# Half of the condition's broadcast row, a fifth raw tile, and gate sums by halves

## The chip, the cores and the metric

The kernel runs on one core of a Trainium2 chip. Its time is the device time of one execution in microseconds (us); with more than one run, the median counts. A core has a matrix engine (PE in the profile), a vector engine (DVE), a scalar engine (ACT), a fourth engine (POOL) and an engine that here only issues transfers (SP). Each takes its instructions in the order of the program; they wait for one another through semaphores. Transfers that SP and POOL issue run on DMA engines beside them.

## The reference

One layer of an encoder: 512 positions, 2048 channels, float32. The condition `c` gives three rows of 2048 numbers (shift, scale, gate); the normalised input, scaled and shifted, goes through one large projection whose columns feed a windowed attention with 16 heads (`aq` to `ag`) and a gated linear attention (GLA) with 4 heads (`gq` to `gg`). Both are gated by a SiLU, joined, projected, multiplied by the gate row, added to the input and normalised. Cut to what matters here:

```python
mod = jax.nn.silu(c) @ w_cond[layer] + b_cond[layer]
shift, scale, gate = jnp.split(mod, 3, axis=-1)
h = rms_norm(x) * (1.0 + scale[:, None]) + shift[:, None]
proj = h @ w_in[layer]
aq, ak, av, ag, gq, gk, gv, gg, lr_f, lr_b = jnp.split(proj, PROJ_SPLITS, axis=-1)
...
a_out = att.reshape(B, S, ATT_WIDTH) * jax.nn.silu(ag)
...
g_out = g_o * jax.nn.silu(gg)
y = jnp.concatenate([a_out, g_out], axis=-1) @ w_out[layer]
x = x + gate[:, None] * y
return rms_norm(x) * final_gain
```

Two kinds of sums over 2048 channels matter for this case. The gate row is `silu(c) @ w_cond` for its 2048 columns. And where the shift goes through the projection of `ag`, it gives a row of its own, `shift @ W_ag`, a bias of 1024 numbers. Both are matrix times vector, and the kernel computes them on the vector engine, not on PE.

## The kernel before

The order of PE's instructions is written out by hand; a scheduler orders those of the other four engines. Every product in float32 is made of three matmuls of a high and a low part (L215 to L217: high by high, low by high, high by low), so each block of weights is loaded as raw float32, its high part is taken on ACT (`split_hi`, L442) and its low part on DVE (`split_lo`, L428).

**Stages.** A first stage reads the condition's weights and the first columns of the projection, and makes shift and scale on DVE with sums against `sb`, a tile of 128 partitions by 2048 that holds silu(c) in every partition. `sb` then stays for the gate sums, and near the end the finished gate row is loaded into the same tile. After the first stage the projection runs in units: qk2, qk4, qk6, gk, gv0, gv1, ag0, ag1, gg0, gg1. Each unit has eight blocks of weights (`qk65` is block 5 of unit qk6, `ag11` block 1 of ag1) and 64 ticks of six matmuls, and carries side work on the way: attention heads in the qk units and gk, GLA heads in gv1, ag0, ag1 and gg0 (heads 0 to 3). The out projection follows, from about 783 us on, in products of halves (`O` blocks).

**Side work of an attention head** (h, i: head and quarter, so s91 is quarter 1 of head 9): score on PE into a PSUM tile (L730, L731); on DVE the bias is added and the row's smallest value found (L734); exp on ACT (L737); reciprocal on DVE (L738); normalisation on POOL (L742); four transposes on PE (L754) into a PSUM tile; their high and low part on ACT (L758) and DVE (L759); values on PE (L768), added up by ACT (L771) and DVE (L775, `cat`). Scores, transposes, values and all GLA products draw PSUM tiles in turn from one ring of three (`PA`), so that each PE product waits until the reader of the tile three products back is done. t90 takes the tile of s91.

**Side work of a GLA head** (h, d: head and direction): z on PE (L869), gates on DVE and ACT (L875 to L899, ending in `ki` L898 and `qi` L899), transposes `kt` (L908), products `kv` (L920), states (L927, L932), attention (L947), mask (L952, L954), outputs `go` (L969), squares `gsq` (L974), their high part `gsh` on ACT (L981) and low part `gsl` on DVE (L982), the norm `gn` on PE (L983, L984), and the result `cat` on DVE (L992). At the end of a unit of ag or gg its four PSUM tiles are gated on DVE (L1052, L1050).

**The sums.** 16 of them give the bias (`rawv{m}{z}`, m 0 to 7) and 32 the gate (`rawg{m}{z}`, m 0 to 15), with z the half of the 2048 channels: each loads 512 KB from SP (L838, L804) and is one instruction on DVE (L843 for the bias' first half, L314 for the rest) that multiplies the raw tile by a broadcast row (`shb` for the bias, `sb` for the gate) and adds up. The sum of z = 1 goes on from the result of z = 0. `SUMS_IN` says how many run in which unit; `some_sums` puts the load of each a little ahead of its place. `masked` makes a gate sum wait, in the order, for the last mask (L954).

**Raw tiles.** The weight blocks (L359), the bias sums and the gate sums all take their raw tile from one ring of four (`RAW`, 128 x 1024). A load can start when the sum, or both splits, of the block four places back are done.

**Transfers of POOL.** Sums of blocks of the output weights are made in DRAM: `T<-in_w_o` and `T<-T` (L391), 512 KB each, of which some copy and some add. They are paced along the units.

Of the kernel before, what the change touches and what calls it, by code (L numbers as in the profile page):

```python
# [10 lines left out]
F32 = mybir.dt.float32  # L11
# [3 lines left out]
ALU = mybir.AluOpType  # L15
# [3 lines left out]
P = 128  # L19
S = 512  # L20
D = 2048
KT = D // P
# [89 lines left out]
GLA_AT = (0.01, 0.02, 0.33, 0.46, 0.46, 0.56, 0.64, 0.76, 0.76, 0.88)  # L112
GLA_FIRST = 0.2

SUMS_IN = {"qk6": 4, "gk": 4, "gv0": 9, "gv1": 2, "ag0": 7, "ag1": 9, "gg0": 9}


OUT_ORDER = ("P1", "P7", "P6", "P4", "P5", "P3", "P2")
# [60 lines left out]
def block_kernel(ctx: ExitStack, tc: tile.TileContext, a: dict):  # L179
    nc = tc.nc  # L180
    cst = ctx.enter_context(tc.tile_pool(name="cst", bufs=1))
# [3 lines left out]
    mid = ctx.enter_context(ExitStack())  # L185
    t2 = mid.enter_context(tc.tile_pool(name="t2", bufs=16))
    gp = mid.enter_context(tc.tile_pool(name="gp", bufs=2))
    sm = mid.enter_context(tc.tile_pool(name="sm", bufs=4))
    pp = ctx.enter_context(tc.tile_pool(name="pp", bufs=4, space=PSUM))
    dp = ctx.enter_context(tc.tile_pool(name="dp", bufs=1, space=DRAM))  # L190
    ctx.enter_context(tc.manual_schedule(engines={E.PE}))

    def T2(name, dt=F32, parts=P):
        return t2.tile([parts, 512], dt, tag="t2", name=name)
# [4 lines left out]
    def PJ(name):  # L199
        return pp.tile([P, 512], F32, tag="pj", bufs=5, name=name)  # L200
# [5 lines left out]
    tt = nc.vector.tensor_tensor  # L206
# [20 lines left out]
    bcond = cst.tile([P, 48], F32, tag="bcond", name="c_bcond")  # L227
# [17 lines left out]
    def RAW(name, shape):  # L245
        return wp.tile([P] + shape, F32, tag="raw", bufs=4, name=name)
# [18 lines left out]
        c = slice(512 * z, 512 * z + 512)  # L265
        nc.sync.dma_start(start_w["a", 0][:, c], a["w_sa"][0, :, 0, c])

    sb = cst.tile([P, 2048], F32, tag="sb", name="sb")
    hot = T2("hot", F32R)
    onesr = cst.tile([P, P], F32R, tag="ones", name="ones")  # L270
    ones = onesr.bitcast(F32)
# [40 lines left out]
    def cond_sum(dst, w, with_, init):  # L312

        nc.vector.tensor_tensor_reduce(out=w, in0=w, in1=with_, op0=ALU.mult, op1=ALU.add,  # L314
                                       scale=1.0, scalar=init, accum_out=dst)
# [98 lines left out]
    def block_sums(name):  # L414
        n = SUM_OPS_IN[name]
        r = [sum_ops.pop(0) for _ in range(n)]
        return [((q + 0.5) / n, x) for q, x in enumerate(r)]
# [13 lines left out]
    def split_hi(i):  # L431
        if i < len(groups) and i not in wts:
            fetch(i)
            u, g = groups[i]
            raw = raws[i].rearrange("p k c -> p (k c)")
            dst = None
            if (u, g) == ("O", len(groups) - gi["O", 0] - 4):
                t = b8.tile([P, 2, 1024], F32R, tag="b8", name="wlast")
                dst = t[:, 0, :], t[:, 1, :]
            wts[i] = dst or (wp.tile([P, 1024], F32R, tag="whi", name=f"{u}{g}h"),  # L440
                             wp.tile([P, 1024], F32R, tag="wlo", name=f"{u}{g}l"))
            last["hi"] = act(wts[i][0], raw, AF.Copy).ins  # L442
# [182 lines left out]
    for z in range(2):  # L625
        for e in range(3):
            name = ("mm", "a", 0, 7) if (z, e) == (1, 2) else ("m0", z, e)
# [3 lines left out]
    for i in range(n):  # L631
        if i > 7:
            mm_task(i)
        st, k, j = chain[i]
# [15 lines left out]
    for i in range(n, 2 * n):  # L650
        mm_task(i)
        st, k, j = chain[i]
# [3 lines left out]
    for w in range(4):  # L656
        for kt in range(4):
            j, g = w // 2 * 4 + kt, w % 2
# [20 lines left out]
    gate = cst.tile([P, KT], F32, tag="gate", name="gate")  # L679
    gate0 = cst.tile([P, KT], F32, tag="gate0", name="gate0")  # L680
# [117 lines left out]
    def gate_half(m, z):  # L798

        t = []  # L800

        def load():
            t.append(RAW(f"rawg{m}{z}", [1024]))
            nc.sync.dma_start(t[0], a["wg"][m, z])  # L804

        def go():
            raw = t[0]

            with tc.issue_after(masked[-1]) if masked else nullcontext():
                if z == 0:  # L810
                    cond_sum(gate0[:, m:m + 1], raw, sb[:, :1024], bcond[:, 32 + m:33 + m])
                else:
                    cond_sum(gate[:, m:m + 1], raw, sb[:, 1024:], gate0[:, m:m + 1])
        return load, go

    masked = []
# [15 lines left out]
    def bias_half(m, z):  # L832

        t = []

        def load():
            t.append(RAW(f"rawv{m}{z}", [1024]))
            nc.sync.dma_start(t[0], a["wv"][m, z])  # L838

        def go():  # L840
            raw = t[0]
            if z == 0:
                nc.vector.tensor_tensor_reduce(out=raw, in0=raw, in1=shb[0][:, :1024], op0=ALU.mult, op1=ALU.add,  # L843
                                               scale=1.0, scalar=0.0, accum_out=vbias0[:, m:m + 1])
            else:
                cond_sum(vbias[:, m:m + 1], raw, shb[0][:, 1024:], vbias0[:, m:m + 1])
        return load, go

    sum_work = [bias_half(m, z) for m in range(8) for z in range(2)]
    sum_work += [gate_half(m, z) for m in range(KT) for z in range(2)]  # L850

    def some_sums(name):
        r = [sum_work.pop(0) for _ in range(SUMS_IN.get(name, len(sum_work)))]
        n = len(r)
        loads = [(max(q - 0.3, 0.1) / n, x[0]) for q, x in enumerate(r)]
        return sorted(loads + [((q + 0.7) / n, x[1]) for q, x in enumerate(r)], key=lambda x: x[0])
# [144 lines left out]
    def urgent(go):  # L1001
        with tc.high_priority(offset=20):
            go()
# [3 lines left out]
    def unit(name, natural, side=(), lr=None):  # L1007
        side = sorted(spill + list(side) + block_sums(name), key=lambda x: x[0])
        spill[:] = [(at - 1, go) for at, go in side if at >= 1]
        side = [x for x in side if x[0] < 1]  # L1010
        ps = [PJ(f"ps_{name}_{i}") for i in range(4)]
        pos, tick, ticks = 0, 0, 64
        for g in range(KT // 2):
            i0 = gi[name, g]
            split_hi(i0)
            split_hi(i0 + 1)
            for ahead in (2, 3):
                fetch(i0 + ahead)
            split_lo(i0)
            hi, lo = wts[i0]  # L1020
            for i in range(4):
                for kk in range(2):
                    k = 2 * g + kk
                    rh, rl = h_hi[:, k, :], h_lo[:, k, :]
                    if natural:
                        t = slice(i * P, i * P + P)
                        cw = slice(kk * 512, kk * 512 + 512)
                        three(ps[i], rh[:, t], rl[:, t], hi[:, cw], lo[:, cw], k == 0, k == KT - 1)
                    else:
                        c = slice(kk * 512 + i * P, kk * 512 + i * P + P)  # L1030
                        three(ps[i], hi[:, c], lo[:, c], rh, rl, k == 0, k == KT - 1)
                    tick += 1
                    if tick % 8 == 2:
                        split_lo(i0 + 1)
                    while pos < len(side) and side[pos][0] * ticks <= tick:
                        urgent(side[pos][1])
                        pos += 1
                if lr is not None:
                    lr(4 * g + i)
        while pos < len(side):  # L1040
            urgent(side[pos][1])
            pos += 1
        return ps
# [9 lines left out]
        lnexp()  # L1053


    for p in range(2):
        qk_evict(p, psb["b", 4 + 2 * p], psb["b", 5 + 2 * p])
    for n, p in (("qk2", 0), ("qk4", 2), ("qk6", 4)):
        ps = unit(n, False, attention((p, p + 1)) + ([(0.05, shift_row)] + some_sums(n) if p == 4 else []))
        for q in range(2):  # L1060
            qk_evict(p + 2 + q, ps[2 * q], ps[2 * q + 1])

    ps = unit("gk", False, attention((6, 7)) + some_sums("gk"))
    gla["k"] = B8("gkt", [4, 512])
    for i in range(4):
        act(gla["k"][:, i, :], ps[i], AF.Copy)
# [18 lines left out]
    ps = unit("gv0", True, some_sums("gv0"), lr=lr_tick)  # L1085
# [20 lines left out]
    ps = unit("gv1", True, gla_head(0) + some_sums("gv1"))  # L1106
# [3 lines left out]
    for j in range(2):  # L1110
        ps = unit(f"ag{j}", False, gla_head(1 + j) + some_sums(f"ag{j}"))
        gate_evict(ps, cat[j], f"a{j}", vbias[:, 4 * j:4 * j + 4])
    ps = unit("gg0", False, gla_head(3) + some_sums("gg0"))
# [43 lines left out]
    ps = unit("gg1", False, side + some_sums("gg1"))  # L1157
# [4 lines left out]
    op = ctx.enter_context(tc.tile_pool(name="op", bufs=1, reuse_waits="tile"))  # L1162
    for e in "hl":
        t = hp.tile([P, KT, 512], F32R, tag="h", name="c_" + e)
        for z, n in enumerate(("S2", "A22", "S1", "S4")):
            ops.setdefault(n, []).append(
                t[:, 4 * z:4 * z + 4, :].rearrange("p k (two c) -> p (k two) c", two=2))

    def gate_row():

        pg = PA("pgate")
        nc.tensor.transpose(pg[:KT, :P], gate, ident)
        gt_ = E_("gatet")
        act(gt_[:KT, :P], pg[:KT, :P], AF.Copy)
        garow = dp.tile([KT, P], F32, tag="garow", name="garow")
        nc.sync.dma_start(garow, gt_[:KT, :P])
        nc.sync.dma_start(sb, bass.AP(garow.tensor, garow.offset, [[0, P], [1, D]]))

    def E_(name):
        return op.tile([P, 512], F32, tag="e", bufs=3, name=name)  # L1180
# [33 lines left out]
    def add_up(i, j, merge, gain):  # L1214

        x_ = xo[i, j]
        t = E_(f"y{i}{j}")
        merge(t)
        tt(t, t, sb[:, 512 * j:512 * j + 512], op=ALU.mult)
        tt(x_, t, x_, op=ALU.add)  # L1220
        act(t, x_, AF.Square, accum_out=ssq[:, i, j:j + 1])
        if gain:
            tt(x_, x_, fgain[j], op=ALU.mult)
# [204 lines left out]
```

## Time and profile before

| | us |
|---|---|
| median of 3 runs | 942.63 (942.31 to 943.21) |
| the profiled execution | 940.34 |
| its span in the profile | 938.6 |
| granted PE clock, mean | 0.994 |
| DVE, gate sums with `sb`, 16 + 16 | 20.5 + 20.5 busy, 1283 ns each |
| idle on DVE ahead of them | 31.1 + 19.1, nearly all for DMA |
| DVE, bias sums, 8 + 8 | 9.8 + 10.3 busy |
| idle on DVE ahead of them | 16.0 + 15.0, all for DMA |
| HBM read and written | 200.53 MB and 37.83 MB |

The profile is one execution. In its views a row has a start in us from the span's start, a duration, the engine, the line, the operation, and tiles written and read with buffer numbers left out; in square brackets stands the idle time ahead of it and what ended it. In the view of waits a row gives who waited for whom, the total, how often, and the longest. The chain of waits follows the execution back from its end, at each step to what released it. In the DMA views the last number is the time from issue to landing. A row of a stretch gives the stretch, its length, busy time and count of PE, PEld (weight loads), DVE, ACT and POOL, then the granted PE clock, the DMA share and GB/s.

### The profile page before, as it was taken

Reading aid. Unit: us, or ns where it says so; the run is one execution under the profiler, and the core shown is the slowest. Engines: PE = TensorE matmul, PEld = TensorE weight load, DVE = VectorE, ACT = ScalarE, POOL = GpSimd, SP = SyncE. Lnnn points to the kernel's source line nnn. Section 1 sums busy time; section 2 is a strip of 40 time slices with the busy share of each in tenths; the row PEclk is TensorE's granted clock in tenths of the full one; section 3 lists DMA queues with packets and bytes.
Section 4 is the critical chain, followed back from the end, with each engine's and each line's share of the span. In section 5 each row is a group of like instructions: output and inputs, shape, how many; then the busy total and the mean of one; then the engine's idle time right before and its main releaser. Section 6 shows DMA issues by size and latency. Waiting matters only on the chain.

```text
span 938.6 us, 12129 instructions
## 1 busy us (share of the span) xinstructions
PE 917.5 (98%) x4375; PEld 760.8 (81%) x4375; DVE 654.6 (70%) x960; ACT 472.2 (50%) x770; POOL 98.3 (10%) x152
## 2 busy tenths in 40 slices
PE   7999999999999999999999999989989999999996
PEld 6888888888888888888877888878878888888884
DVE  7988899766755676766444657476686639697496
ACT  5553533565655645655413545363643428555464
POOL 0000000012222122122000100111002000000001
PEclk9999999999999999999999999999999999999998
DMA  9999497465765775755656546666766567856743
GB/s 352 404 412 383 166 372 269 158 199 148 188 198 153 217 234 166 239 167 147 209 200 197 162 151 221 202 199 199 247 209 200 187 195 267 315 203 217 276 179 135
DMA packets 54339, 209.79 MB, mean 224 GB/s; under 512 B 7204, under 2 KB 7492, under 8 KB 45960
## 3 DMA queue, kind: packets, MB, share of 16 engines
q1 hardware_dynamic: 48656, 174.83, 51.1%
q0 software_dynamic: 5184, 33.62, 15.1%
q8 instruction: 34, 0.56, 0.2%
q10 hardware_dynamic: 440, 0.57, 0.2%
q14 instruction: 25, 0.20, 0.1%
HBM read 200.53 MB, written 37.83 MB: 254 GB/s over the span
## 4 chain that ended last, share of the span: by engine, by line
PE 81%; DMA 8%; DVE 7%; issue 3%; ACT 1%; POOL 0%; SPq 0%; DVEq 0%; POOLq 0%; ACTq 0%
DMA rawg<-in_wg 5%; PE ps_qk L215 4%; PE ps_qk L217 4%; PE ps_qk L216 4%; PE g L217 4%; PE g L215 4%; PE g L216 4%; PE stb L217 3%; PE stb L216 3%; PE stb L215 3%; PE o L768 3%; PE ps_gv L217 3%; PE ps_gv L216 3%; PE ps_gv L215 3%; PE t L754 3%
## 5 line engine op out<-in xcount | busy, mean ns | idle before, releaser
L737 ACT ACTIVATE p<-p,st 128x512 f32<-128x512 f32 x64 | 46.1, 720 | 56.3 <-DVE st L734 55.9
L314 DVE CUSTOM_DVE_ANT_0 cb<-cb,sb,c_bcond 128x2048 f32<-128x2048 f32 (+1 forms) x32 | 73.4, 2295 | 1.3 <-DMA cb<-in_wm 1.0
L391 POOL DMA_DIRECT2D T<-in_w_o x48 | 33.5, 704 | 311.3 <-ACT qk21h L442 119.8
L742 POOL TENSOR_SCALAR p<-p,st 128x512 f32<-128x512 f32 x62 | 43.2, 697 | 196.1 <-DVE st L738 152.9
L759 DVE TENSOR_TENSOR pt<-t,pt 128x512 fp32r<-128x512 f32 x64 | 43.7, 688 | 15.6 <-ACT pt L758 15.4
L734 DVE CUSTOM_DVE_ANT_0 p<-s,g 128x512 f32<-128x512 f32 x64 | 43.6, 686 | 13.7 <-PE s L731 13.4
L758 ACT ACTIVATE pt<-t 128x512 fp32r<-128x512 f32 x64 | 37.8, 591 | 9.9 <-PE t L754 8.9
L314 DVE CUSTOM_DVE_ANT_0 rawg<-rawg,sb,gate 128x1024 f32<-128x1024 f32 x16 | 20.5, 1283 | 31.1 <-DMA rawg<-in_wg 30.9
L754 PEld LDWEIGHTS t<-c_ident,p 128*128 128x128 f32 x256 | 31.5, 140 | 9.7 <-POOL p L742 1.4
L754 PE MATMUL t<-c_ident,p 128*128 128x128 f32 x256 | 38.5, 273 | 0.1
L768 PEld LDWEIGHTS o<-pt,vv 128*128 128x128 f32 x256 | 34.8, 188 | 2.8
L768 PE MATMUL o<-pt,vv 128*128 128x256 f32 x256 | 35.5, 281 | 0.0
L314 DVE CUSTOM_DVE_ANT_0 rawg<-rawg,sb,c_bcond 128x1024 f32<-128x1024 f32 x16 | 20.5, 1282 | 19.1 <-DMA rawg<-in_wg 19.0
L738 DVE RECIPROCAL st<-st 128x1 f32<-128x1 f32 x64 | 10.3, 161 | 24.9 <-ACT p L737 24.9
L730 PE MATMUL s<-ks,qs 128*128 128x512 f32 x64 | 25.1, 392 | 0.2 <-DVE cat L775 0.2
L731 PE MATMUL s<-kl,qs 128*128 128x512 f32 x64 | 25.0, 391 | 0.0
L937 ACT ACTIVATE sq<-st,sc 128x256 f32<-128x256 f32 x24 | 12.2, 508 | 22.1 <-DVE st L927 13.0
L843 DVE CUSTOM_DVE_ANT_0 rawv<-rawv,shb 128x1024 f32<-128x1024 f32 x8 | 9.8, 1225 | 16.0 <-DMA rawv<-in_wv 16.0
L314 DVE CUSTOM_DVE_ANT_0 rawv<-rawv,shb,vbias 128x1024 f32<-128x1024 f32 x8 | 10.3, 1282 | 15.0 <-DMA rawv<-in_wv 15.0
L1253 POOL TENSOR_SCALAR x<-x,rn 128x512 f32<-128x512 f32 x3 | 3.4, 1137 | 158.4 <-ACT rn L1242 158.4
L771 ACT ACTIVATE oh<-o 64x256 f32<-64x256 f32 x32 | 12.2, 382 | 13.7 <-PE o L768 12.7
L775 DVE TENSOR_TENSOR cat<-o,oh 64x256 f32<-64x256 f32 x32 | 13.3, 416 | 7.6 <-ACT oh L771 7.2
(1520 smaller groups left out, 2978.0 us busy)
## 6 DMA issues: line engine op xcount, KB each, us to landing
cb<-in_wm SPq DMA_DIRECT2D x31, 1024.0 KB, 8.5
T<-in_w_o POOLq DMA_DIRECT2D x48, 512.0 KB, 5.2
rawg<-in_wg SPq DMA_DIRECT2D x32, 512.0 KB, 4.6
raw_O<-T SPq DMA_DIRECT2D x32, 512.0 KB, 5.0
raw_qk<-in_w_qk SPq DMA_DIRECT2D x24, 512.0 KB, 3.3
raw_O<-in_w_o SPq DMA_DIRECT2D x24, 512.0 KB, 4.2
rawb<-in_w_sb SPq DMA_DIRECT2D x16, 512.0 KB, 4.9
T<-T POOLq DMA_DIRECT2D x16, 512.0 KB, 3.6
```

The source lines that it names most:

```text
L215: mm(ps, lh, rh, start=first, stop=False, skip_group_check=more)
L216: mm(ps, ll, rh, start=False, stop=False, skip_group_check=more)
L217: mm(ps, lh, rl, start=False, stop=last, skip_group_check=more)
L314: nc.vector.tensor_tensor_reduce(out=w, in0=w, in1=with_, op0=ALU.mult, op1=ALU.add, scale=1.0, scalar=init, accum_out=dst)
L391: move = nc.gpsimd.dma_start(dst, src, max_dma_last_dim=8192, **how).ins
L734: nc.vector.tensor_tensor_reduce(out=t, in0=ps, in1=gt[h][:, P * i:P * i + 512], op0=ALU.add, op1=ALU.min, scale=1.0, scalar=3e38, accum_o ...
L737: act(t, t, AF.Exp, bias=st[:, 0:1], scale=-1.0, accum_out=st[:, 1:2])
L742: last["pool"] = nc.gpsimd.tensor_scalar(t, t, st[:, 2:3], 1.0, op0=ALU.mult, op1=ALU.mult).ins
L754: nc.tensor.transpose(pk[:, kt * P:kt * P + P], t[:, kt * P:kt * P + P], ident)
L758: act(hi, src, AF.Copy)
L759: tt(lo, src, hi.bitcast(F32), op=ALU.subtract)
L768: mm(po[:, :256], vv[h // 4][:, kt, h % 4, :], t[:, w, kt, :], start=kt == 0 and w == 0, stop=kt == 3 and w == 1)
```

## The change

`sb` moves into a pool of its own that is closed after the first stage. Before that, its first partition is written to DRAM as a row of 2048 (`cond_row`, one 8 KB transfer). The space then goes to a pool with two tiles of 128 x 1024, tagged "l" and "h". Half z of the row is loaded as a broadcast of 512 KB when it is wanted: `crow0` into "l" in the unit gk, `crow1` into "h" with the load of gate sum (13, 0). The other tile of the two is a raw tile in the meantime:

- the bias sums of z = 1 use "h" and no longer the ring of four;
- the gate sums run all z = 0 first, then all z = 1. Those of odd m use the free tile: "h" for z = 0 up to m = 11, "l" for z = 1. The others stay in the ring.

`SUMS_IN` has three sums in gv1 instead of two and eight in ag1 instead of nine, and the finished gate row gets a tile in the pool of the output stage (`gate_b`). The order of instructions on PE and POOL is the same in both programs; on DVE, ACT and SP the scheduler's order differs.

```diff
-SUMS_IN = {"qk6": 4, "gk": 4, "gv0": 9, "gv1": 2, "ag0": 7, "ag1": 9, "gg0": 9}
+SUMS_IN = {"qk6": 4, "gk": 4, "gv0": 9, "gv1": 3, "ag0": 7, "ag1": 8, "gg0": 9}
...
+    first = mid.enter_context(ExitStack())
+    sbp = first.enter_context(tc.tile_pool(name="sbp", bufs=1))
...
-    sb = cst.tile([P, 2048], F32, tag="sb", name="sb")
+    sb = sbp.tile([P, 2048], F32, tag="sb", name="sb")
...
         def load():
-            t.append(RAW(f"rawg{m}{z}", [1024]))
+            if m % 2 and (z or m < 12):
+                t.append(two.tile([P, 1024], F32, tag="lh"[1 - z], name=f"rawg{m}{z}"))
+            else:
+                t.append(RAW(f"rawg{m}{z}", [1024]))
             nc.sync.dma_start(t[0], a["wg"][m, z])
+            if (m, z) == (13, 0):
+                cond_half(1)
...
-                    cond_sum(gate0[:, m:m + 1], raw, sb[:, :1024], bcond[:, 32 + m:33 + m])
+                    cond_sum(gate0[:, m:m + 1], raw, crow[0], bcond[:, 32 + m:33 + m])
                 else:
-                    cond_sum(gate[:, m:m + 1], raw, sb[:, 1024:], gate0[:, m:m + 1])
+                    cond_sum(gate[:, m:m + 1], raw, crow[1], gate0[:, m:m + 1])
...
-            t.append(RAW(f"rawv{m}{z}", [1024]))
+            t.append(two.tile([P, 1024], F32, tag="h", name=f"rawv{m}{z}") if z else RAW(f"rawv{m}{z}", [1024]))
...
-    sum_work += [gate_half(m, z) for m in range(KT) for z in range(2)]
+    sum_work += [gate_half(m, z) for z in range(2) for m in range(KT)]
...
+    cond_row = dp.tile([1, 2048], F32, tag="cond_row", name="cond_row")
+    nc.sync.dma_start(cond_row, sb[0:1, :])
+    first.close()
+    two = mid.enter_context(tc.tile_pool(name="two", bufs=1, reuse_waits="tile"))
+    crow = {}
+
+    def cond_half(z):
+        crow[z] = two.tile([P, 1024], F32, tag="lh"[z], name=f"crow{z}")
+        nc.sync.dma_start(crow[z], bass.AP(cond_row.tensor, cond_row.offset + 1024 * z, [[0, P], [1, 1024]]))
...
-    ps = unit("gk", False, attention((6, 7)) + some_sums("gk"))
+    ps = unit("gk", False, attention((6, 7)) + [(0.5, lambda: cond_half(0))] + some_sums("gk"))
...
+    gate_b = op.tile([P, 2048], F32, tag="gate", name="gate_b")
...
-        nc.sync.dma_start(sb, bass.AP(garow.tensor, garow.offset, [[0, P], [1, D]]))
+        nc.sync.dma_start(gate_b, bass.AP(garow.tensor, garow.offset, [[0, P], [1, D]]))
...
-        tt(t, t, sb[:, 512 * j:512 * j + 512], op=ALU.mult)
+        tt(t, t, gate_b[:, 512 * j:512 * j + 512], op=ALU.mult)
```

## The prediction

> **What bounds the kernel now.** I read the page first, then the waits of TensorE, its timeline around each wait, and last the chain of waits.
>
> ```profile
> PE 917.5 (98%) x4375; PEld 760.8 (81%) x4375; DVE 654.6 (70%) x960; ACT 472.2 (50%) x770; POOL 98.3 (10%) x152
> PE 81%; DMA 8%; DVE 7%; issue 3%; ACT 1%; POOL 0%; SPq 0%; DVEq 0%; POOLq 0%; ACTq 0%
> ```
>
> TensorE is busy for 98% of the span, and the change gives it neither more nor less to do: it runs the same instructions in the same order. Only its waits can move. The view of waits, for TensorE, lists these behind the start-up:
>
> ```profile
> PE kt L908 <- DVE ki L898: 3.1, 1, 3.1
> PE z L869 <- DVE cat L992: 2.9, 1, 2.9
> PE s L730 <- DVE cat L775: 0.2, 1, 0.2
> PE gn L984 <- DVE gsl L982: 0.2, 1, 0.2
> ```
>
> Two waits of 3 us and crumbs: the most that can be won is small, and one new wait of that size outweighs it. TensorE's timeline at the second, and the same stretch in the view by windows, show that such a wait costs more than itself:
>
> ```profile
> 616.29 0.39 PE L216 MATMUL ps_ag<-h_hi,ag10l 128*128 128x512 f32 x1
> 616.52 0.39 PE L217 MATMUL ps_ag<-h_lo,ag10h 128*128 128x512 f32 x1
> 619.81 0.76 PE L869 MATMUL z<-lrst,ups 128*128 128x512 f32 x1 [2.90 <-DVE cat L992]
> ...
> 622.92 0.39 PE L215 MATMUL ps_ag<-h_hi,ag10h 128*128 128x512 f32 x1
> ```
> ```profile
> 619.00:623.00 4.00, 3.19 (x8) 2.55 (x9) 4.00 (x8) 1.05 (x2) 0.77 (x1) 0.57 0.81 209
> ```
>
> Matmuls start 0.23 us apart; the next was due at 616.75 and came at 619.81, 3.06 late. The seven matmuls from there to 622.92 take 3.11 us where 7 x 0.23 = 1.6 is normal, at a granted clock of 0.57 (the column behind the five engines). So this wait cost 3.06 + 1.5 = 4.6 us, and I price the one at kt L908 alike: 3.1 + 1.5 = 4.6.
>
> Who made z wait is in the chain of waits, and VectorE's own waits show that it is a habit:
>
> ```profile
> 603.12 7.43 DMA rawg<-in_wg
> ...
> 611.89 5.68 DMA rawg<-in_wg
> 617.71 1.28 DVE rawg L314
> 619.00 1.32 DVE cat L992 x2
> ```
> ```profile
> DVE rawg L314 <- DMA rawg<-in_wg: 50.0, 18, 5.7
> ```
>
> VectorE works in order. A gate sum waits for its 512 KB; the product `cat` (L992) stands behind it, and z, which needs cat's PSUM buffer, behind that. The load went out at 611.89 only because one of the four raw buffers had just come free. A fifth tile lets such loads go earlier. That is the gain; the price is that the scheduler's order on VectorE changes with it, and where a sum now stands is what I cost below. All times are those of the profile of before; a stall shifts what follows on all engines alike, so each part is worked out in its own stretch.
>
> **Part A: the bias sums take the single tile "h".** Each second half of a bias sum (`rawv{m}1`) now lands in one tile, so its load leaves when the second half before it has been summed. In the changed program's order on VectorE, the sum of rawv11 stands directly behind the cat of o80 (342.87 below) and ahead of the score p91 (343.20); before, it stood two scores later, at 350.44.
>
> ```profile
> 338.18 1.28 DVE L314 CUSTOM_DVE_ANT_0 rawv<-rawv,shb,vbias 128x1024 f32<-128x1024 f32 x1
> ...
> 342.87 0.40 DVE L775 TENSOR_TENSOR cat<-o,oh 64x256 f32<-64x256 f32 x1
> 343.20 0.67 DVE L734 CUSTOM_DVE_ANT_0 p<-s,g 128x512 f32<-128x512 f32 x1
> ...
> 350.44 1.28 DVE L314 CUSTOM_DVE_ANT_0 rawv<-rawv,shb,vbias 128x1024 f32<-128x1024 f32 x1 [2.30 <-DMA rawv<-in_wv]
> ```
> ```profile
> 345.95 0.60 PE L754 MATMUL t<-c_ident,p 128*128 128x128 f32 x4
> ...
> 352.12 0.49 PE L730 MATMUL s<-ks,qs 128*128 128x512 f32 x1 [0.25 <-DVE cat L775]
> ```
>
> The sum that frees "h" (rawv01) ends at 338.18 + 1.28 = 339.46, so rawv11's load leaves at about 339.5: on SP's queue that is the place of raw_qk67, which left at 339.50. What that place is worth, SP's and POOL's timelines and the DMA issues between 336 and 352 us show, with the page's median of a rawg load beside them:
>
> ```profile
> 339.50 0.33 SPq L359 DMA_DIRECT2D raw_qk<-in_w_qk  x1
> ```
> ```profile
> 337.28 0.81 POOL L391 DMA_DIRECT2D T<-in_w_o  x1
> ```
> ```profile
> raw_qk<-in_w_qk SPq DMA_DIRECT2D x1, 512.0 KB, 8.3
> g<-grow SPq DMA_DIRECT2D x1, 448.0 KB, 8.9
> ```
> ```profile
> rawg<-in_wg SPq DMA_DIRECT2D x32, 512.0 KB, 4.6
> ```
>
> POOL had issued a paced sum in DRAM two microseconds earlier, and the load behind it took 8.3 us. With that, rawv11 lands at 347.8, its sum takes 1.28, the score 0.67: p91 is read at 349.75. Queued behind it are TensorE's transposes t90 (345.95), which overwrite the PSUM buffer of the score s91: 3.8 us late. That is longer than both old waits, so I add their 1.5 us at half clock, and take off the old 0.25 at 352.12, whose sum is gone from there: **+5.05**. Bounds: with 4.6 us, the page's median, it lands at 344.1, p91 ends at 346.0 and nothing waits, -0.25; with the 8.9 of the row beside it, +5.7. I take 8.3 since it is the same place in the same queue.
>
> [...]
>
> The bias sum rawv21 moves likewise, ahead of the product pt110 and the score p113:
>
> ```profile
> 378.30 0.15 DVE L738 RECIPROCAL st<-st 128x1 f32<-128x1 f32 x1
> ...
> 379.70 0.69 DVE L734 CUSTOM_DVE_ANT_0 p<-s,g 128x512 f32<-128x512 f32 x1 [0.34 <-PE s L731]
> ```
> ```profile
> 382.53 0.66 PE L754 MATMUL t<-c_ident,p 128*128 128x128 f32 x4
> ```
>
> It adds 1.28 behind 378.30; 0.34 of it falls into an idle stretch, so p113 is 0.94 late, and its exp, normalisation and transposes (382.53) with it. With some 0.2 of slack I take **+0.75**, between 0 and 0.94. The other bias sums move inside stretches where the next TensorE wait is over 2 us off: nothing, unless their loads too take 8 us.
>
> **Part B: first gate head boundary, 596 to 620.** With all first halves in a row and one more tile, VectorE's order is: sums 8, 9, 10, ag10l, sum 11, gsq, **sum 12**, gsl, ag11l, cat. Before, no sum stood between gsq and gsl, and cat waited for two loads.
>
> ```profile
> 606.68 0.69 DVE L982 TENSOR_TENSOR gsl<-gsq,gsh 128x512 fp32r<-128x512 f32 x1 [0.70 <-ACT gsh L981]
> ```
> ```profile
> 610.15 0.39 PE L984 MATMUL gn<-gsl,ones 128*128 128x512 f32 x1
> ```
>
> The old wait goes: cat has only ag11l between it and gsl and ends over 3 us before z is due, -4.6. But sum 12's load takes the place of the rawg load that left at 603.12 and landed at 610.55 (chain of waits above), so gsl ends at 610.55 + 1.28 + 0.69 = 612.5, and gn, due at 610.15, waits 2.3. Net **-2.3**. Bounds: a load that lands by 608 gives -4.6; with half clock behind the 2.3 us it is -0.8.
>
> **Part D: boundary at 655 to 702.** The last sum ahead of ki L898 stood between ki30 and ki31; it now stands ahead of ki30, and gg05l moves behind ki31.
>
> ```profile
> 687.20 1.28 DVE L314 CUSTOM_DVE_ANT_0 rawg<-rawg,sb,c_bcond 128x1024 f32<-128x1024 f32 x1
> ...
> 692.72 1.28 DVE L314 CUSTOM_DVE_ANT_0 rawg<-rawg,sb,gate 128x1024 f32<-128x1024 f32 x1 [0.63 <-DMA rawg<-in_wg]
> ...
> 696.53 1.23 DVE L428 TENSOR_TENSOR gg05l<-raw_gg,gg05h 128x1024 fp32r<-128x1024 f32 x1 [0.65 <-ACT gg05h L442]
> ```
> ```profile
> 689.29 0.49 PE L908 MATMUL kt<-c_ident,ki 128*128 128x128 f32 x3
> ```
>
> Sum (1.28 + 0.63) and gg05l (1.23 + 0.65) leave the stretch ahead of ki31: 3.8 us, more than the 3.1 it was late, so that wait goes, -4.6. The sum's 1.28 + 0.63 = 1.9 now comes ahead of ki30, whose kt (689.29) had no slack: +1.9, spread over gn, kt30 and kt31. Net **-2.7**; bounds -4.6 (the earlier load hides it) and, with half clock, -1.2.
>
> **Part E: third boundary, 715 to 730.** Sum rawg121 now stands ahead of the last gsl.
>
> ```profile
> 720.91 0.33 SPq L804 DMA_DIRECT2D rawg<-in_wg  x1
> ```
> ```profile
> rawg<-in_wg SPq DMA_DIRECT2D x1, 512.0 KB, 7.3
> ```
> ```profile
> 727.77 0.39 PE L984 MATMUL gn<-gsl,ones 128*128 128x512 f32 x1
> ```
>
> A load issued here (the second row is that of the issues from 718 to 722 us) took 7.3. One tile more sends it one sum's length (1.28) earlier, 719.6; it lands at 726.9, sum and gsl (1.28 + 0.69) end at 728.9, gn waits **+1.1**. Bounds: with 4.6 us nothing, at the old 720.91 it is 2.4.
>
> **The rest costs nothing:** two 512 KB broadcasts (crow0 in the gk unit, crow1 in ag1) are two more rawg-sized loads of 4.6 us; they are wanted tens of microseconds later, and if that cover went they would push a load by one such length. The 8 KB row store likewise. The final gate row lands in its own tile instead of `sb`; the products that read it run in the output stage, where TensorE has no wait.
>
> Sum: 5.05 + 0.75 - 2.3 - 2.7 + 1.1 = **+1.9 us** on the profiled execution's own 940.34 (span 938.6): 942.2. That execution lies 2.3 below the median of the runs, 942.63, so the forecast is 942.63 + 1.9 = **944.5**.
>
> **The rivals.**
> *Faster: rawv11 is there in time.* One mechanism, at 342.87 on VectorE: if its load takes up to 4.6 us, part A falls from +5.05 to -0.25, and the sum is -3.4: **939.2**. For it: the page's median. Against: the 8.3 of that place. It decides at a landing of 344.1; every microsecond beyond costs one.
> *Slower: loads behind POOL's sums take 8.9 us everywhere.* Then A is 5.7; in B the load, 1.5 later, makes gn wait 3.8 and brings half clock, -4.6 + 5.3 = +0.7; D is -1.2 and E 1.1 + 1.6 = 2.7. With 0.75 that is +8.7, **951.3**; half way to it from the forecast, as likely, is 948. For it: the 8.9, and the new positions, all of which stand ahead of work that TensorE wants. Against: most rawg loads take 4.6.
> *The change does not do what it says.* Loads still leave when a sum frees a tile, sums come as late as before, and B and D win nothing while A and F are paid: 942.63 + 5.8 = **948.4**. For it: 18 waits for rawg, 50 us in all, that one tile cannot cover. Against: one load more in flight is worth a sum's 1.28 plus its wait.
>
> **How the numbers follow.** Forecast 0.42 (942.5 to 946.5), faster rival 0.24, slower 0.24, nothing won 0.10. A measurement of this kernel tells about 0.2%, 1.9 us, from no change, and the forecast lies on that line: half of it, 0.21, counts as slower. With the slower rival and the case of nothing won that is 0.55, less 0.09 for their mild ends (a shorter A above all): slower 0.46. The same has the other half and those 0.09, 0.30; faster is its rival's 0.24. The forecast's own range is 942.5 to 946.5. The range, 938.5 to 949, takes in the faster rival's price and the milder half of the slower one's.
>
> **What would show it.** Right: a wait of some 4 us of t L754 near 346, behind p L734 and a rawv sum, with a slow run behind it; z L869 and the long kt L908 gone from TensorE's waits; gn L984 with 1 to 2.3 us twice. Wrong: no wait near 346 (A), z or kt still 3 us (B, D), a wait in the output stage or at the first gate sums (broadcasts), or half clock missing behind a wait of 3.8 us.

## The result, and the profile after

The changed kernel takes 947.69 us in the median of 5 runs (946.21 to 948.98), the kernel before 942.63 us (940.50 to 944.13): a ratio of 1.0056, 95% interval 1.0037 to 1.0075. It is slower by half a percent. The profiled executions are 947.69 us (span 945.9) and 940.34 us (span 938.6); the latter lies 2.3 us below its median, so the two profiles differ by 7.35 us where the medians differ by 5.1. What follows compares the profiles.

TensorE's waits after, behind the start-up (who waited for whom: total, times, longest):

```profile
PE gn L991 <- DVE gsl L989: 5.4, 3, 2.1
PE t L756 <- DVE st L736: 3.5, 1, 3.5
...
PE t L756 <- DVE pt L761: 0.8, 1, 0.8
PE kv L927 <- DVE st L939: 0.8, 1, 0.8
PE kt L915 <- DVE ki L905: 0.7, 1, 0.7
```

The waits of z and kt that stood here before are gone or down to 0.7, and t and gn stand in their place. Line numbers are those of the changed kernel: 2 more than before in the attention heads, 7 more in the GLA heads. The gate sums themselves wait less for their loads than before (page of the changed kernel, costliest groups; the last figures are the idle time ahead of the group and what ended it):

```profile
L316 DVE CUSTOM_DVE_ANT_0 rawg<-rawg,crow,gate 128x1024 f32<-128x1024 f32 x16 | 20.4, 1282 | 22.5 <-DMA rawg<-in_wg 22.5
L316 DVE CUSTOM_DVE_ANT_0 rawg<-rawg,crow,c_bcond 128x1024 f32<-128x1024 f32 x16 | 20.4, 1282 | 21.2 <-DMA rawg<-in_wg 21.2
```

Ended by a load, that is 43.7 us of idle time against 49.9 before (30.9 + 19.0): the loads are better covered, yet TensorE waits longer, so what stands behind the remaining waits must have changed.

Where the first 5 us come from is seen on VectorE and TensorE in the unit qk6 (timelines of the changed kernel):

```profile
341.83 0.40 DVE L777 TENSOR_TENSOR cat<-o,oh 64x256 f32<-64x256 f32 x1
347.32 1.28 DVE L316 CUSTOM_DVE_ANT_0 rawv<-rawv,shb,vbias 128x1024 f32<-128x1024 f32 x1 [5.08 <-DMA rawv<-in_wv]
348.53 0.08 DVE L316 DVE_READ_ACCUMULATOR2_ANT vbias<- 128x1 f32 x1
348.53 0.68 DVE L736 CUSTOM_DVE_ANT_0 p<-s,g 128x512 f32<-128x512 f32 x1
```
```profile
345.48 0.40 PE L219 MATMUL ps_qk<-h_lo,qk63h 128*128 128x512 f32 x1
349.37 1.08 PE L756 MATMUL t<-c_ident,p 128*128 128x128 f32 x4 [3.49 <-DVE st L736]
...
354.52 0.56 PE L217 MATMUL ps_qk<-h_hi,qk63h 128*128 128x512 f32 x1
```
```profile
339.26 0.33 SPq L845 DMA_DIRECT2D rawv<-in_wv  x1
```
```profile
346.00:356.00 10.00, 6.63 (x24) 5.84 (x25) 5.49 (x12) 2.49 (x6) 2.92 (x3) 0.66 0.53 168
```

The third view is SP's timeline, the fourth the stretch by windows. VectorE idles 5.08 us for the load of rawv11, which left at 339.26 and whose sum could start 8.06 us later; the score p91 comes behind the sum, the transposes t90 behind the score. TensorE waits 3.49 us and then runs at half clock until about 354.9 (0.66 over the ten microseconds).

The n-th matmul of one profile is the n-th of the other, 4375 in both, so their starts can be subtracted. The difference after minus before stays level for long stretches and jumps at a few places; these jumps are the whole change between the two profiles:

| place (us, before) | what | jump (us) | forecast |
|---|---|---|---|
| 345 to 355 | t90 behind the sum of rawv11 | +6.19 - 0.53 | +5.05 |
| 380 to 385 | the sum of rawv21, head 11 | +1.43 | +0.75 |
| 445 to 450, 555 to 560 | small waits come and go | +0.49 - 0.69 | 0 |
| 610 to 625 | gn waits, z no longer | +2.15 - 4.62 | -2.3 |
| 665 to 710 | gn and kv wait, kt hardly | +1.71 + 1.08 - 3.93 | -2.7 |
| 725 to 735 | gn waits | +4.01 | +1.1 |
| all, with -0.3 in crumbs elsewhere | | +7.0 | +1.9 |

The two outer boundaries differ in an instructive way. TensorE's timeline after, at the first and the last gn, and the last one's stretch by windows:

```profile
618.78 0.50 PE L991 MATMUL gn<-gsl,ones 128*128 128x512 f32 x1 [1.83 <-DVE gsl L989]
```
```profile
733.09 0.51 PE L991 MATMUL gn<-gsl,ones 128*128 128x512 f32 x1 [2.13 <-DVE gsl L989]
733.66 0.53 PE L218 MATMUL ps_gg<-h_hi,gg07l 128*128 128x512 f32 x1
...
736.98 0.49 PE L217 MATMUL ps_gg<-h_hi,gg07h 128*128 128x512 f32 x1
```
```profile
731.00:739.00 8.00, 5.91 (x19) 4.71 (x20) 6.69 (x9) 4.34 (x7) 0.53 (x1) 0.79 0.70 266
619.00:623.00 4.00, 4.00 (x18) 3.27 (x18) 2.65 (x4) 3.61 (x6) 0.00 (x0) 1.00 0.91 346
```

Both wait some 2 us. Behind the last one eight matmuls run at half clock (0.79 over eight microseconds, 0.21 x 8 = 1.7 us lost); behind the first, none (1.00). What tells them apart isn't shown; the last section has more such pairs.

### The profile page after: what moved, and what is told of

Same layout as the page of the kernel before. It is cut to its first block, busy times and chain, and to the rows that moved or that the text cites. A ratio compares the mean times of both kernels' runs of the same rounds, so it can differ in the third digit from the quotient of the medians.

```text
span 945.9 us, 12130 instructions
## 1 busy us (share of the span) xinstructions
PE 920.1 (97%) x4375; PEld 761.9 (81%) x4375; DVE 655.3 (69%) x960; ACT 471.9 (50%) x770; POOL 98.6 (10%) x152
## 4 chain that ended last, share of the span: by engine, by line
PE 78%; DMA 8%; DVE 7%; issue 3%; ACT 2%; POOL 0%; SPq 0%; DVEq 0%; POOLq 0%; ACTq 0%
DMA rawg<-in_wg 5%; PE ps_qk L217 4%; PE ps_qk L218 4%; PE ps_qk L219 4%; PE g L219 4%; PE g L217 4%; PE g L218 4%; PE stb L219 3%; PE ps_gv L219 3%; PE ps_gv L218 3%; PE ps_gv L217 3%; PE stb L218 3%; PE stb L217 3%; PE o L770 3%; PE sta L218 2%
## 5 line engine op out<-in xcount | busy, mean ns | idle before, releaser
L736 DVE CUSTOM_DVE_ANT_0 p<-s,g 128x512 f32<-128x512 f32 x64 | 43.7, 687 | 14.2 <-PE s L733 14.0
L316 DVE CUSTOM_DVE_ANT_0 rawg<-rawg,crow,gate 128x1024 f32<-128x1024 f32 x16 | 20.4, 1282 | 22.5 <-DMA rawg<-in_wg 22.5
L316 DVE CUSTOM_DVE_ANT_0 rawg<-rawg,crow,c_bcond 128x1024 f32<-128x1024 f32 x16 | 20.4, 1282 | 21.2 <-DMA rawg<-in_wg 21.2
L508 ACT ACTIVATE h_hi<-xt,shift 128x512 fp32r<-128x512 f32 x16 | 11.5, 719 | 13.0 <-DVE shift L316 13.0
```

Of the source, the lines that this page charges most:

```text
L736: nc.vector.tensor_tensor_reduce(out=t, in0=ps, in1=gt[h][:, P * i:P * i + 512], op0=ALU.add, op1=ALU.min, scale=1.0, scalar=3e38, accum_o ...
```

## The experiments

My theory: a sum whose load is late holds up what the scheduler has put behind it on VectorE, so the *places* of the sums cost, and the tile as such helps. Rivals: the single tile makes loads late wherever their sums stand; the change costs by its extra transfers; a wait only ever moves to the next thing in VectorE's order; POOL's adding transfers make the loads late. Ratios are to the kernel before, timed among the same runs; the changed kernel's is 1.0056.

| run | what it changes | median (us) | ratio, 95% interval |
|---|---|---|---|
| e1_ring | bias sums back in the ring | 941.86 | 0.9988 (0.9964 to 1.0011) |
| e2_norm | gate sums behind gsl | 946.64 | 1.0039 (1.0020 to 1.0058) |
| e3_both | both of these | 939.53 | 0.9951 (0.9928 to 0.9974) |
| e4_noadd | no adding in DRAM | 936.94 | 0.9941 (0.9919 to 0.9964) |
| e5_order | bias sums behind a score | 939.60 | 0.9955 (0.9938 to 0.9971) |
| e7_halves | kernel before, order by halves | 942.28 | 0.9984 (0.9962 to 1.0005) |
| e8_early | ring, more sums early | 945.08 | 1.0024 (1.0005 to 1.0042) |
| e9_earlynorm | the same, gate sums behind gsl | 947.98 | 1.0055 (1.0031 to 1.0079) |
| e10_beforeearly | kernel before, more sums early | 949.76 | 1.0067 (1.0038 to 1.0096) |
| e11_mild | behind a score, one sum less in ag1 and gg0 | 939.46 | 0.9959 (0.9942 to 0.9976) |
| e12_pin3 | behind a score, three sums behind gsl | 936.93 | 0.9942 (0.9919 to 0.9966) |
| e13_ki | the same, and one sum behind ki | 938.69 | 0.9961 (0.9943 to 0.9979) |

**Bias sums back in the ring.** The gate sums and their loads are held behind the last bias sum and load, since they would run much earlier otherwise.

```diff
-            t.append(two.tile([P, 1024], F32, tag="h", name=f"rawv{m}{z}") if z else RAW(f"rawv{m}{z}", [1024]))
-            nc.sync.dma_start(t[0], a["wv"][m, z])
+            t.append(RAW(f"rawv{m}{z}", [1024]))
+            loaded.append(nc.sync.dma_start(t[0], a["wv"][m, z]).ins)
...
+            with tc.issue_after(loaded[-1]):
+                nc.sync.dma_start(t[0], a["wg"][m, z])
...
+                masked.append(cond_sum(vbias[:, m:m + 1], raw, shb[0][:, 1024:], vbias0[:, m:m + 1]).ins)
```

> The changed kernel with one part undone: the bias sums of z = 1 take their raw tile from the ring of four again (the gate sums are held behind the last bias sum and their loads behind the last bias load, so that they stay where the changed kernel has them). If the bias sums in the single tile cost what the profile shows at 345 to 355 us (+5.7), at 380 to 385 (+1.4) and at 445 to 450 (+0.5), this run is 7.6 us faster than the changed kernel's 947.7: about 940, and the wait of t L756 of 3.5 us is gone. If the extra transfers or the new place of the tiles slow the kernel, little changes: 946 to 948.

0.9988 / 1.0056 = 0.993, so 6.4 us faster than the changed kernel, and the wait of t is gone. The extra transfers (crow, the row store) are still in, so they cost nothing that shows. TensorE's waits in this run:

```profile
PE gn L992 <- DVE gsl L990: 4.3, 3, 1.7
PE kv L928 <- DVE st L940: 1.8, 1, 1.8
```

**The bias sums keep their tile, but stand behind a score.** `scored` holds the scores' instructions on VectorE (L736) as they were traced.

```diff
-                    cond_sum(vbias[:, m:m + 1], raw, shb[0][:, 1024:], vbias0[:, m:m + 1])
+                with tc.issue_after(scored[-1]):
+                    cond_sum(vbias[:, m:m + 1], raw, shb[0][:, 1024:], vbias0[:, m:m + 1])
```

> The changed kernel with its single tile for the bias sums of z = 1, but each such sum held on DVE behind the score traced last before it; the sum of rawv11 then stands behind p92 again, as in the kernel before, while its load still leaves when rawv01's sum frees the tile. If the place ahead of p91 is what costs, the wait of t L756 near 350 us goes (5.7 us), and most of the 1.4 at 385: 941 to 942.5. If the late load of the single tile costs wherever the sum stands, a wait of 2 us or more comes back at the next score or cat: 944 to 947.

939.60 us, 1% below the changed kernel and under the 941 to 942.5 expected, and the wait of t near 350 us is gone: the single tile as such doesn't cost, when its sums stand behind the scores. VectorE's timeline shows p91 and p92 ahead of a bias sum, which finds its data there:

```profile
341.29 0.42 DVE L778 TENSOR_TENSOR cat<-o,oh 64x256 f32<-64x256 f32 x1 [0.24 <-ACT oh L774]
342.54 0.69 DVE L737 CUSTOM_DVE_ANT_0 p<-s,g 128x512 f32<-128x512 f32 x1 [0.83 <-PE s L734]
...
345.35 0.68 DVE L737 CUSTOM_DVE_ANT_0 p<-s,g 128x512 f32<-128x512 f32 x1
345.96 1.28 DVE L316 CUSTOM_DVE_ANT_0 rawv<-rawv,shb,vbias 128x1024 f32<-128x1024 f32 x1
```

That sum isn't rawv11's, though. It is the first of z = 1 in this run: the edge holds rawv01's sum back too, from 337.95 in the changed kernel to 345.96. So rawv11's load leaves at 347.28 and no longer at 339.26, and its sum, at 379.47, finds its data as well (SP's timeline, then VectorE's):

```profile
347.28 0.33 SPq L846 DMA_DIRECT2D rawv<-in_wv  x1
```
```profile
379.47 1.27 DVE L316 CUSTOM_DVE_ANT_0 rawv<-rawv,shb,vbias 128x1024 f32<-128x1024 f32 x1
```

The expectation had the early load stay; it didn't. The rival that the single tile makes sums late wherever they stand is out, but the run moves the load together with the sum, and doesn't tell the two apart. With this one edge in the order the change is faster than the kernel before (0.9955).

**All gate sums behind gsl, alone and with the ring.**

```diff
-            tt(lo, sq, hi.bitcast(F32), op=ALU.subtract)
+            masked.append(tt(lo, sq, hi.bitcast(F32), op=ALU.subtract).ins)
```

> The changed kernel with the gate sums that are traced behind a head's norm held behind that head's gsl on DVE. If the three waits of gn (5.4 us in all, and 1.7 of half clock behind the last) come from sums that stand ahead of gsl, they go, and the run is about 7 us faster than 947.7: 941; the sums behind gsl then stand ahead of cat and ki, and 1 to 2 us may come back there: 941 to 943. The rival, that a sum's wait only moves to the next thing behind it on DVE (cat, and with it z and kt as before), gives 946 to 949.

> Both edits together. If the two losses are independent, they add up: 947.7 - 7.6 - 7 = 933 to 936, 7 to 9 us faster than the kernel before. If what limits is the number of loads that can be on their way, the waits come back at cat and ki: 940 to 943.

For the pin alone the rival was right. No gn waits any more in either, but kt does; the first row is of the run with the pin alone, the second of the run with both edits:

```profile
PE kt L915 <- DVE ki L905: 4.1, 1, 4.1
```
```profile
PE kt L916 <- DVE ki L906: 6.8, 2, 4.0
```

The sums that may not run ahead of gsl come later, and one of them now stands directly ahead of ki, where it waits 4.39 us for its load in the run with the pin alone. Of the 7 us hoped for, 1.6 are left by the ratios (946.64); together with the ring it is 939.53, between the two expectations (933 to 936 and 940 to 943). Its runs scatter from 932.87 to 943.47, and the one with a profile is the slowest of the twelve, so its 6.8 us of kt are not the usual case; whether the two long waits are missing in the faster executions isn't shown.

**No adding in DRAM.** The accumulating transfers of POOL become copies of the same size, so the sums of output weights are left out.

```diff
-            paced(dsum[pair, name, g], flat(out_block(pair, OUT_SUMS[name][1], g)), accum_op=ALU.add)
+            paced(dsum[pair, name, g], flat(out_block(pair, OUT_SUMS[name][1], g)))
```

> The changed kernel with POOL's adding transfers in DRAM made plain copies of the same size (the sums of output weights are left out, so the output is another one); all orders are the same. If a load takes 7 to 8.5 us because it runs beside an adding transfer, loads land after 3 to 5 us, and the waits of t L756 (3.5) and of gn (5.4) shrink to under 1 each with no half clock: 936 to 940. If the loads are late for another reason (their place in SP's queue, HBM), 946 to 948 and the waits stay.

The time is as expected (936.94), and for gn so is the reason: its waits fall from 5.4 to 0.3 us. At the last of them the load of rawg121 takes 6.6 us where it took 8.4, and POOL's transfer that left 0.99 us ahead of it takes 5.8 as a copy where it took 8.8 as an add. For t the reason holds only in part. The load of rawv11 left at 338.36 and its sum could start 6.84 us later, against 8.06 in the changed kernel (timelines of VectorE and SP, then TensorE's waits):

```profile
345.20 1.28 DVE L316 CUSTOM_DVE_ANT_0 rawv<-rawv,shb,vbias 128x1024 f32<-128x1024 f32 x1 [3.86 <-DMA rawv<-in_wv]
```
```profile
338.36 0.33 SPq L845 DMA_DIRECT2D rawv<-in_wv  x1
```
```profile
PE t L756 <- DVE st L736: 2.3, 1, 2.3
...
PE gn L991 <- DVE gsl L989: 0.3, 1, 0.3
```

So the adding accounts for 1.2 of these 8 us. Other transfers are in flight in both runs (the DMA engines are busy for 0.90 of 339 to 348 in the changed kernel, and still for 0.70 of 338 to 347 here); which of them the rest is due to, no run tells. A wait of 2.3 instead of 3.5 is worth more than 1.2, since it comes without the half clock: the mean granted clock is 0.998 in this run and 0.991 in the changed kernel. That is how small shifts of a landing become microseconds.

**More sums early, three ways.** The sums by unit become 14, 8, 5, 4, 4, 5 (gv0 to gg1): on the ring run, on the ring run with the pin, and on the kernel before.

```diff
-SUMS_IN = {"qk6": 4, "gk": 4, "gv0": 9, "gv1": 3, "ag0": 7, "ag1": 8, "gg0": 9}
+SUMS_IN = {"qk6": 4, "gk": 4, "gv0": 14, "gv1": 8, "ag0": 5, "ag1": 4, "gg0": 4}
```

> The run with the bias sums in the ring, with more gate sums early: 14 sums in gv0, 8 in gv1, 5 in ag0, 4 each in ag1 and gg0, 5 in gg1. At a head's boundary three or four sums stand instead of six. If the waits of gn, kt and kv (6.9 us in that run) come from the number of sums that want their loads at the boundary, they shrink to under 2: 936 to 938, 4 to 6 us faster than with the old distribution. If a single sum behind an adding transfer is enough for them, 940 to 942.

> The same distribution with gate sums held behind gsl as well. With few sums at a boundary there is less to pile up ahead of ki, so the 6.8 us at kt go too: 934 to 937, the fastest so far. If the pile ahead of ki remains, 940 to 943.

> The kernel before with that distribution alone: the whole row resident, four raw tiles, sums in the old order m by m. DVE's order has the sums at nearly the same places as the run with five tiles. If the fifth tile is what lets sums land in time, this run keeps waits of 2 to 3 us at gn, z or kt: 940 to 942, 3 or more slower than with five tiles. If the places of the sums decide and not the tile, it comes out with the five-tile run within 2 us.

No gn waits any more in the first two, as the theory has it, but new waits come where the sums went (first run of the three, then the kernel before with the same numbers):

```profile
PE kt L916 <- DVE ki L906: 4.7, 1, 4.7
PE t L756 <- ACT p L742: 3.5, 1, 3.5
PE z L877 <- DVE ups L1121: 2.3, 1, 2.3
```
```profile
PE kt L908 <- DVE ki L898: 5.2, 2, 4.4
PE t L754 <- ACT p L740: 3.4, 1, 3.4
PE gn L983 <- ACT gsh L981: 2.7, 1, 2.7
PE gn L984 <- DVE gsl L982: 2.1, 2, 1.9
PE z L869 <- DVE ups L1102: 2.1, 1, 2.1
```

I was wrong that gv0 and gv1 had room, and all three runs are slower than expected. In the first run a bias sum stands ahead of the last score's reciprocal (450 us), and gate sums stand ahead of `ups` (523) and of ki30's counterpart of head 0 (539), with 3.09, 6.90 and 5.28 us idle for their loads. The run with the pin besides is no better (947.98 where 934 to 937 was expected): there kt waits 6.2 us, t 3.0 and z 2.3. Five tiles (1.0024) beat four (1.0067), as expected in sign, by 4 to 5 us in the medians; the intervals overlap a little. The first gate head's boundary shows the tile at work: a sum stands ahead of gsq in both, with five tiles its load leaves at 610.98 and lands ahead of it, with four it leaves at 616.63 behind an add of POOL's, the sum waits 8.31 us and gn 2.7. At the last boundary it is the order again: with four tiles a sum stands between gsq and gsl (737.88) and gn waits 1.9, with five none stands there. So the 4 to 5 us aren't the price of the tile alone.

**Only the three sums right ahead of a gsl.** On top of the bias sums behind a score.

```diff
+            after = normed if (m, z) in ((12, 0), (4, 1), (12, 1)) else masked
-            with tc.issue_after(masked[-1]) if masked else nullcontext():
+            with tc.issue_after(after[-1]) if after else nullcontext():
...
-            tt(lo, sq, hi.bitcast(F32), op=ALU.subtract)
+            normed.append(tt(lo, sq, hi.bitcast(F32), op=ALU.subtract).ins)
```

> The run with the bias sums held behind a score, and besides only the three gate sums that stand right ahead of a gsl (rawg120, rawg41, rawg121) held behind it. If a single sum ahead of gsl is what gn waits for, the 2.7 us of gn go to under 1 and nothing grows, as no more than one sum moves at each boundary: 936.5 to 938. If it piles up at ki as it did when all sums were held, kt waits 3 us more somewhere: 940 to 944.

936.93 us, 0.9942: the fastest of the runs that compute the whole layer, 0.6% below the kernel before and 1.1% below the changed one, though its interval overlaps that of the run without the three pins (0.9955). gn no longer appears among TensorE's waits; kt grew by 1.9 against the run without this edit (1.5 there), so part of it did move:

```profile
PE kt L918 <- DVE ki L908: 3.4, 2, 2.5
...
PE t L757 <- POOL p L745: 1.0, 1, 1.0
...
PE kv L930 <- DVE st L942: 0.8, 1, 0.8
```

**Two variations of it.** One sum less in ag1 and gg0, without the three pins (10, 3, 7, 7, 8, 5); and the three pins with rawg61 behind ki30 as well.

> The run with the bias sums held behind a score, with one sum moved from ag1 and one from gg0 to gv0 and gg1 (10, 3, 7, 7, 8, 5). One sum less at the boundary of head 1 and another order there: if the number of sums at a boundary decides, gn falls by about 1 us: 937.5 to 939. If the waits near 452, 523 and 539 us that came with 14 and 8 sums already begin with one more sum in gv0, 941 to 944.

> The fastest run so far (bias sums behind a score, three gate sums behind gsl) with rawg61 held behind ki30 as well, ahead of which it stands where kt30 waits 2.5 us. If the sum ahead of ki30 is what kt30 waits for, that wait falls by the sum's 1.3 to about 1, kt31's 0.9 stays under 2.2, and the run is 1 us faster: 935 to 937. If the sum only moves the wait to kt31, no change: 936.5 to 938.

Neither beats it beyond doubt: 0.9959 and 0.9961, with intervals that overlap 0.9942 to 0.9966. In the first, gn waits 2.4 us in one place, and the mean granted clock is 0.995 where the run without this edit has 0.997. In the second the wait of kt30 did fall, but kt31's grew and another kt waits, 4.3 us in all: the wait moved, as the second expectation had it, and the 938.69 us are a little over the 936.5 to 938 that went with it.

**Halves alone, on the kernel before.**

```diff
-    sum_work += [gate_half(m, z) for m in range(KT) for z in range(2)]
+    sum_work += [gate_half(m, z) for z in range(2) for m in range(KT)]
```

> The kernel before with the gate sums by halves alone: all z = 0 first, then all z = 1, with the whole row resident, four raw tiles and the old numbers of sums by unit. DVE's order keeps its places, only the names of the sums change, so it should tell nothing from the kernel before: 941 to 944 and the same two waits (z, kt) of about 3 us. If the halves themselves cost something, over 945.

0.9984, its interval holds 1, and VectorE's order has the sums at the same places: the order by halves alone costs nothing that shows.

## Why the prediction came out as it did

The direction, the wide range (938.5 to 949) and most of the mechanism held; the size was too small, +1.9 forecast where the medians differ by 5.1 and the profiles by 7.35, and 947.69 lies outside the forecast's own 942.5 to 946.5. Step by step:

- *A sum of rawv11 ahead of p91 holds up t90* (+5.05): 5.7 measured, with 8.06 us from the load's issue to its sum (8.3 assumed) and half clock behind it. Two runs show it by its undoing: with the ring the wait goes, and with the bias sums behind a score it goes while the tile stays (the load then leaves later too). The reason given for the 8 us, POOL's sum in DRAM, was mostly wrong: without adding 6.84 of 8.06 remain.
- *rawv21* (+0.75): 1.4. The lateness went on to two more transposes.
- *B* (-2.3): -2.5. z's wait left, gn waits 2.
- *D* (-2.7): **misread and mis-sized**, -1.1. The old wait was worth 3.9, not 4.6. The forecast put the extra sum ahead of ki30 and expected one late sum ahead of a gsl at the first and the last boundary, but not here. VectorE's timeline of the changed kernel has one at this boundary too, rawg41's:

```profile
668.17 0.69 DVE L981 TENSOR_TENSOR gsq<-gsq,gsq 128x512 f32<-128x512 f32 x1 [0.19 <-ACT gsq L978]
672.68 1.28 DVE L316 CUSTOM_DVE_ANT_0 rawg<-rawg,crow,gate 128x1024 f32<-128x1024 f32 x1 [3.82 <-DMA rawg<-in_wg]
673.90 0.68 DVE L989 TENSOR_TENSOR gsl<-gsq,gsh 128x512 fp32r<-128x512 f32 x1
```

  gn waits 1.44 for it, and not when it is pinned behind gsl. kt30, one of the three over which the forecast spread its 1.9, doesn't wait, and directly ahead of ki30 one sum stands in both kernels; kt31 waits 0.65, and kv, which was not on the list, 0.80: 2.9 in all where 1.9 was assumed.
- *E* (+1.1): the step that failed worst, 4.0. The sum stands where it was forecast:

```profile
726.23 0.68 DVE L981 TENSOR_TENSOR gsq<-gsq,gsq 128x512 f32<-128x512 f32 x1
731.14 1.28 DVE L316 CUSTOM_DVE_ANT_0 rawg<-rawg,crow,gate 128x1024 f32<-128x1024 f32 x1 [4.23 <-DMA rawg<-in_wg]
732.35 0.69 DVE L989 TENSOR_TENSOR gsl<-gsq,gsh 128x512 fp32r<-128x512 f32 x1
```

  Its load's time was right too (rawg121 left at 722.56, which is 719.5 in the time of before, where 719.6 was assumed), but the load took longer than the 7.3 it was given, as the DMA issues from 722 to 724 us of the changed kernel show:

```profile
T<-in_w_o POOLq DMA_DIRECT2D x1, 512.0 KB, 8.8
rawg<-in_wg SPq DMA_DIRECT2D x1, 512.0 KB, 8.4
```

  One microsecond more of lateness made a wait of 2.13, and this one was followed by half clock (0.79 over 731 to 739) that cost 1.7 us, which the forecast gave only to waits of 3 us. In the two runs that changed only the bias sums (ring, order) the same gn lost 2.3 and 3.3 us less, at a mean granted clock of 0.997 in both (0.991 in the changed kernel), although nothing was changed there. It isn't when the load leaves: in all three it leaves 0.99 us behind the same add of POOL. But that add took 8.8, 7.3 and 6.5 us, and the load 8.4, 7.8 and 6.8; without adding it was 5.8 and 6.6, and the jump at this gn was 0.6 instead of 4.0. So the load is late with the add. Why the add's own time differs between executions stays open, so how late it is, and whether half clock follows, was luck here as far as the runs show.
- *The rest costs nothing*: right, by the ring run.

The rival "loads take 8.9 everywhere" described A and E best; its price of +8.7 was near the 7.35 between the profiles, but its B (+0.7) didn't come. The case of nothing won gave 948.4, nearest to the measured time, and only by luck: z's wait left and B and D did win. (It charges "A and F", and there is no part F; its 5.8 is the two terms of A.)

## What to carry to other kernels

Before a buffer is added, ask which order the scheduler makes of it: a sum that can start earlier is put earlier, and on an engine that works in order its late load then holds up whatever stands behind it (5.08 us idle on VectorE for rawv11, 3.49 on TensorE behind it). Hold such filler work, by an order edge, behind the short steps that the busy engine waits for, a few at a time: held back all together, one of them comes late ahead of the next such step (kt waited 4.1 us). And price a wait of the matrix engine with what follows it, not by its length alone: here waits of 2.13 and 3.49 us were followed by half clock, one of 2.46 us was not.

## What the runs showed of the hardware

A wait's half clock isn't set by its length alone. Counted from one matmul's start to the next, the gap of 2.53 us at the changed kernel's last gn (a wait of 2.13) was followed by matmuls 0.43 us apart, where 0.23 is normal; the granted clock is 0.79 from 731 to 739. The gap of 2.84 us at kt30 in the run with three pins (a wait of 2.46) was not:

```profile
685.36 0.39 PE L219 MATMUL ps_gg<-h_lo,gg02h 128*128 128x512 f32 x1
688.20 0.52 PE L918 MATMUL kt<-c_ident,ki 128*128 128x128 f32 x3 [2.46 <-DVE ki L908]
688.48 0.48 PE L217 MATMUL ps_gg<-h_hi,gg02h 128*128 128x512 f32 x1
688.79 0.39 PE L218 MATMUL ps_gg<-h_hi,gg02l 128*128 128x512 f32 x1
689.02 0.40 PE L219 MATMUL ps_gg<-h_lo,gg02h 128*128 128x512 f32 x1
689.26 0.40 PE L217 MATMUL ps_gg<-h_hi,gg02h 128*128 128x512 f32 x1
```

The other waits of over a microsecond behind the start-up, in the changed kernel and the kernel before:

| place (us) | wait (us) | gap (us) | granted clock |
|---|---|---|---|
| changed kernel, second gn, 674.63 | 1.44 | 1.83 | 1.00 over 672 to 676 |
| changed kernel, first gn, 618.78 | 1.83 | 2.23 | 1.00 over 619 to 623 |
| kernel before, z, 619.81 | 2.90 | 3.29 | 0.57 over 619 to 623 |
| kernel before, kt, 698.41 | 3.14 | 3.53 | 0.57 over 698 to 702 |
| changed kernel, t90, 349.37 | 3.49 | 3.89 | 0.66 over 346 to 356 |

What decides besides the length, the runs don't show.
